# Keys turned in blocks by VectorE and brought to their tokens by GpSimd's transfers, held until the matrix to be inverted has been loaded

## The chip, the cores and the metric

The kernel runs on one core of one Trainium2 chip. A core has five engines that run their own instruction streams in order: TensorE (PE, matmuls, with its weight loads on PEld), VectorE (DVE), ScalarE (ACT), GpSimd (POOL) and SyncE (SP), besides the DMA engines that carry transfers between memories. The metric is the device time of one execution in microseconds (us); a run's verdict is taken from the medians of several executions. The time before is a median of 2228.72 us over 3 runs (2228.09 to 2231.8).

## The reference, cut to what matters

One step of a hybrid backbone: an RMS norm, one wide input projection, a bidirectional RWKV-7 time mixing over 32 heads of size 64 with 128 context and 256 latent tokens, beside it a gated short convolution, then the output projections. The part that the change touches is the time mixing. Per head and direction a 64x64 state S runs over the tokens:

```python
def step(S, inp):
    r_t, w_t, k_t, v_t, a_t, b_t = inp
    sa = jnp.einsum('dbhij,dbhj->dbhi', S, a_t)
    S = S * w_t[..., None, :] + sa[..., :, None] * b_t[..., None, :] + v_t[..., :, None] * k_t[..., None, :]
    y = jnp.einsum('dbhij,dbhj->dbhi', S, r_t)
    return S, y
...
S_fin, ys = _wkv_bidir(S0, _heads(r2), _heads(decay), _heads(k_dir), _heads(v2),
                       _heads(-kk2), _heads(kk2 * a))
```

The kernel doesn't step through single tokens. It cuts the 384 tokens of a direction into chunks of 64, computes within a chunk with matrices of 64x64 (one of them has to be inverted), and carries the state from chunk to chunk.

## The kernel before, in words

Everything large is a dense matmul with the weights read from HBM: 1 MB arrives as a tile `raw` (line 101 on), ACT casts it to a rounded high part `whi` (L88), DVE subtracts to get the low part `wlo` (L89), and each product is three matmuls (L81, L82, L83). The class `Stream` hands these dense steps out one at a time (`ds_.go(n)`, n steps of 3 matmuls).

Between the dense steps stand 16 blocks b, of two heads (128 columns) each. A block runs through `prep_a` (projections of decay and rates), `prep_k` (keys, logarithms of decay, exponentials), `prep_b`, `prep_c`, `scan`, `norm` and `finish`. Each function is a generator, and what it yields is the number of dense steps that PE does at that place (the function `drive`). So PE's order is written out by hand (`tc.manual_schedule` for PE alone). The order of the other engines is chosen by a scheduler when the program is built, from priorities (the scan has 300 more) and its own estimate of when an operand is there. On the chip each engine runs its list in that fixed order.

One block, with its lines:

- `prep_b` multiplies the keys and bonus keys with decays, `bk0`/`bk1` (two DVE products per direction, the lines under L679) and `pr0`/`pr1`. PE makes the chunk matrices `pA` (L708), DVE masks them into `A` (L714). Four corners go out through DRAM (`ui`, L719), come back with one matrix per partition as `un` (L732) and `ux` (L734). The loop at L737 to L742 inverts them on DVE in 30 steps of two instructions each. The inverse goes out (`uo`, L746), into `A` (L752), and is turned to `x11` (L755).
- Meanwhile POOL multiplies `bk` with the end decay (L722), DVE turns the values in 32x32 blocks (`vt`, L727), and `prep_c` brings these blocks with 8 POOL transfers to their tokens, the lower half of `sav` (L777). PE turns the keys with 10 transposes through PSUM (`pb`, L784) and ACT copies them into `bt` (L785, four copies).
- `scan` does `pav`, `pH`, `pX` (L862, L854), which complete the inverse, and then runs two chains over the chunks. One step of a chain is: PE `pq` (L833), ACT copies it into `sav` (L835), PE `pu` with `bt` and `sav` (L840), DVE puts it into the state `st` (L843 for a chain's first step from zero, L845 otherwise), PE `po` from `st` (L816), DVE adds it into `sav` (L817). The chains alternate with 2 or 4 dense steps between.
- Inside the scan, after the copies of `pX` into `A` (L890), the function `keys` calls `prep_k` of the next block: reciprocals (L651), `kn` (L652), two running sums `L_0`, `L_1` (L659), exponentials on ACT (L661, L662), `kd` (L664, L665) and `sig` (L666).

Of the kernel before, what the change touches and what calls it, by code (L numbers as in the profile page):

```python
# [9 lines left out]
F32 = mybir.dt.float32  # L10
F32R = mybir.dt.float32r
AF = mybir.ActivationFunctionType
ALU = mybir.AluOpType
AX = mybir.AxisListType

P = 128
# [5 lines left out]
C = 64  # L22
NCH = 6
# [33 lines left out]
def hybrid_step(ctx, tc, cst, x_prompt, x_sample, state_f, state_b, c, c_ctx, ada_w, ada_b, norm_g,  # L57
# [3 lines left out]
    V, S, G, TE = nc.vector, nc.scalar, nc.gpsimd, nc.tensor  # L61
# [14 lines left out]
    ident = cs[:, C_ID:C_ID + P]  # L76
# [150 lines left out]
    for i in range(3):  # L227
        pr = pp.tile([P, P], F32, tag=f"prow{i}", name=f"prow{i}")
# [24 lines left out]
    def pcol(i, n=1):  # L253
        return par[:, i:i + n]
# [154 lines left out]
    def tmp(nm):  # L409
        return box["sp"].tile([P, T], F32, tag="t", name=nm, bufs=8)  # L410
# [134 lines left out]
    sp = ctx_sc.enter_context(tc.tile_pool(name="sp", bufs=1))  # L545
# [6 lines left out]
    for i in range(3):  # L552
        t = tmp(f"lst_{i}")
# [4 lines left out]
    for m in range(4):  # L558
# [6 lines left out]
        t = tmp(f"lin_{m}")  # L565
# [16 lines left out]
    for i in range(4):  # L582
        ep = sp.tile([P, NCH, C + 1], F32, tag=f"ep{i}", name=f"ep{i}")
# [6 lines left out]
    def bank(nm):  # L590
        return ps1.tile([P, 4, P], F32, tag="A", name=nm, bufs=5)

    def c3(a):
        return a.rearrange("p (n t) -> p n t", t=C)

    def flat(a):
        return a.rearrange("p n t -> p (n t)")
# [11 lines left out]
    ux = sp.tile([112, 16, 32], F32, tag="ux", name="ux")  # L609
# [62 lines left out]
    def prep_b(b, o):  # L672

        r, kk = r_[b], o["kk"]
        o["pr"], o["bk"] = [], []
        for d in range(2):
            ep, em, kd, bn = o["ep"][d], o["em"][d], o["kd"][d], o["bn"][d]
            pr = sp.tile([P, NCH, P], F32, tag=f"pr{d}", name=f"pr_{b}_{d}")
            bk = sp.tile([P, NCH, P], F32, tag=f"bk{d}", name=f"bk_{b}_{d}")  # L679
            V.tensor_tensor(bk[:, :, 0:C], c3(bn[:]), c3(em[:]), ALU.mult)  # L680
            V.tensor_tensor(bk[:, :, C:P], c3(kd[:]), c3(em[:]), ALU.mult)
            V.tensor_tensor(pr[:, :, 0:C], c3(kk[:, ::-1] if d else kk[:]), ep[:, :, 0:C], ALU.mult)
            r3 = c3(r[:])
            if d == 0:
                V.tensor_tensor(pr[:, :, C:P], r3, ep[:, :, 1:C + 1], ALU.mult)
            else:
                V.tensor_tensor(pr[:, :, C:P], r3[:, ::-1, :], ep[:, :, C:0:-1], ALU.mult)
            o["pr"].append(pr)
            o["bk"].append(bk)
        yield PB0  # L690

        def blocks(A, d, e):

            es = slice(32 * e, 32 * e + 32)
            return A[es, 0, NCH * d:NCH * d + NCH, :].rearrange("s n (h t) -> s (n h) t", h=2)[:, :, es]

        ui = dp.tile([2, 2, 12, 32, 32], F32, tag="ui", name=f"ui_{b}", bufs=2)
        uo = dp.tile([2, 2, 12, 32, 32], F32, tag="uo", name=f"uo_{b}", bufs=2)

        A = sp.tile([P, 2, 2 * NCH, P], F32, tag="A", name=f"A_{b}")  # L700
        o["A"] = A
        for d in range(2):
            pr, bk = o["pr"][d], o["bk"][d]
            m0 = C_MB if d else C_MF
            pas = {(h, n0): bank(f"pA_{b}_{d}_{h}_{n0}") for n0 in (0, 4) for h in range(2)}
            for n in range(NCH):
                for h in range(2):
                    TE.matmul(pas[h, n // 4 * 4][:, n % 4, :], bk[hss[h], n, :], pr[hss[h], n, :],  # L708
                              start=True, stop=True)
            for n0, w in ((0, 4), (4, 2)):  # L710
                mk = cs[:, m0:m0 + P].rearrange("p (w t) -> p w t", t=C).unsqueeze(1).broadcast_to([P, w, 2, C])
                for h in range(2):
                    f0 = NCH * d + n0
                    last = V.tensor_tensor(A[:, :, f0:f0 + w, hss[h]].rearrange("p w n t -> p n w t"),  # L714
                                           pas[h, n0][:, 0:w, :].rearrange("p n (w t) -> p n w t", t=C), mk,
                                           ALU.mult).ins
            yield PB1
            for e in range(2):
                nc.sync.dma_start(ui[d, e].rearrange("i s t -> s i t"), blocks(A, d, e))  # L719

        for d in range(2):
            G.tensor_tensor(o["bk"][d][:], o["bk"][d][:], o["ep"][d][:, :, C:C + 1].broadcast_to([P, NCH, P]), ALU.mult)  # L722

        vt = sp.tile([P, 2, T], F32, tag="vt", name=f"vt_{b}")
        with tc.issue_after(last):
            for d in range(2):
                V.transpose(vt[:, d], v_[b][:, ::-1] if d else v_[b][:])  # L727
        o["vt"] = vt


        for g in range(2):
            nc.sync.dma_start(un[64 * g:64 * g + 48], ui[:].rearrange("d e i s t -> (d e i) s t"))  # L732
        for g in range(2):
            nc.sync.dma_start(ux[64 * g:64 * g + 48],  # L734
                              ui[:].rearrange("d e i (m g) t -> (d e i) m g t", g=2)[:, :, g, :])
        ut = sp.tile([112, 128], F32, tag="ut", name=f"ut_{b}")
        for s in range(1, 31):  # L737
            w, m = 31 - s, (s + 1) // 2
            tv = ut[:, 0:m * w].rearrange("p (a b) -> p a b", b=w)
            V.tensor_tensor(tv, ux[:, 0:m, s:s + 1].broadcast_to([112, m, w]),  # L740
                            un[:, s:s + 1, s + 1:].broadcast_to([112, m, w]), ALU.mult)
            V.tensor_tensor(ux[:, 0:m, s + 1:], ux[:, 0:m, s + 1:], tv, ALU.add)  # L742
        for g in range(2):
            dg = ux[64 * g:64 * g + 48].rearrange("p a b -> p (a b)")[:, g:512:34]
            V.tensor_scalar(dg, dg, 1.0, None, ALU.add)
            nc.sync.dma_start(uo[:].rearrange("d e i (m g) t -> (d e i) m g t", g=2)[:, :, g, :],  # L746
                              ux[64 * g:64 * g + 48])
        x11 = un[0:64, 0:24, :]
        o["x11"] = x11
        for e in range(2):  # L750
            for d in range(2):
                nc.sync.dma_start(blocks(A, d, e), uo[d, e].rearrange("i s t -> s i t"))  # L752

        for d in range(2):
            box["turned"] = V.transpose(x11[0:32, 12 * d:12 * d + 12, :], blocks(A, d, 0)).ins  # L755

    def prep_c(b, o):

        r = r_[b]

        s_in = sp.tile([P, 2, C], F32, tag="s_in", name=f"s_in_{b}")
        for d in range(2):
            for h in range(2):
                for jb in range(2):
                    p0 = C * h + 32 * jb
                    nc.sync.dma_start(s_in[p0:p0 + 32, d, :].rearrange("i (b j) -> i b j", j=32),
                                      ctx_st[d][0, 0, 2 * b + h].rearrange("(b i) j -> i b j", i=32)
                                      [:, :, 32 * jb:32 * jb + 32])

        sav = sp.tile([P, 2 * NCH, P], F32, tag="sav", name=f"sav_{b}")  # L770
        bt = sp.tile([P, 2 * NCH, P], F32, tag="bt", name=f"bt_{b}")
        o["sav"], o["bkt"] = sav, bt

        x = o["vt"][:].rearrange("p d (n e t) -> p (d n) e t", e=2, t=32)
        for e in range(2):
            for q in range(4):
                G.dma_start(sav[C + 32 * e:C + 32 * e + 32, :, 32 * q:32 * q + 32], x[32 * q:32 * q + 32, :, e, :])  # L777
        yield 2
        for d in range(2):

            for n0, n1 in (((0, 4), (4, 5)), ((0, 3), (4, 6)))[d]:
                pb = bank(f"pb_{b}_{d}_{n0}")
                for n in range(n0, n1):
                    TE.transpose(pb[:, n - n0, :], o["bk"][d][:, n, :], ident)  # L784
                S.copy(bt[:, NCH * d + n0:NCH * d + n1, :], pb[:, 0:n1 - n0, :])  # L785
                yield 1
        ks = o["kd"]
        V.tensor_tensor(ks[0][:], ks[0][:], ks[1][:, ::-1], ALU.add)
        V.scalar_tensor_tensor(ks[0][:], ks[0][:], pcol(RK + b), r[:], ALU.mult, ALU.mult)
        o["bsum"] = hl_parts(ks[0], sp.tile([P, T], F32R, tag="t", name=f"bsh_{b}", bufs=8), f"bs_{b}")  # L790
        yield 1
        for h in range(2):
            for d in range(2):
                V.transpose(st[1][hss[h], d, hss[h]], s_in[hss[h], d, :])
# [178 lines left out]
    for b in range(NB):  # L973
# [10 lines left out]
        n = drive(prep_c(b, cur))  # L984
# [140 lines left out]
    for half in range(2):  # L1125
# [8 lines left out]
        for s in range(3):  # L1134
# [10 lines left out]
            if half == 1:  # L1145
                f = rsf[:, s, :]
# [37 lines left out]
```

## Time and profile before

| what | value |
|---|---|
| median of 3 runs | 2228.72 us |
| the profiled execution's own time | 2230.84 us |
| its span in the trace | 2229.1 us |
| DVE busy | 1501.9 us (67%) |
| ACT busy | 978.4 us (44%) |
| POOL busy | 200.9 us (9%) |
| start of block 3, of block 4 | 520.83, 625.14 us |

The span is what the trace covers; the execution's own time has another 1.7 us around it. The blocks start at 185.36 us (block 0) and 1773.00 us (block 15), and those from 2 to 14 are 103.7 to 105.5 us apart. Groups of instructions are read as: line, engine, operation, output from input, count, busy time in us, mean ns of one, and idle time of the engine just before them with what ended it.

### The profile page before, as it was taken

How to read it: one execution, taken by the hardware profiler on the slowest of the kernel's cores; microseconds unless marked ns; L12 is line 12 of the kernel's file. 1: busy time of each engine (PE TensorE's matmuls, PEld its weight loads, DVE VectorE, ACT ScalarE, POOL GpSimd, SP SyncE). 2: the span in 40 equal slices, each digit the busy share in tenths (PEclk: the TensorE clock that was granted, in tenths of full speed). 3: DMA queues.
4: the chain of work that ended last, by engine and by line, in shares of the span. 5: the costliest groups of instructions: out<-in, count | busy, mean ns of one | idle time of the engine just before them, and what ended most of it. 6: DMA issues, size and time to landing. Idle time of an engine off the chain costs nothing.

```text
span 2229.1 us, 40796 instructions
## 1 busy us (share of the span) xinstructions
PE 2168.6 (97%) x15924; PEld 2056.5 (92%) x15924; DVE 1501.9 (67%) x3288; ACT 978.4 (44%) x1704; POOL 200.9 (9%) x243
## 2 busy tenths in 40 slices
PE   6999999999999999999999999999999999999998
PEld 3588999999999999999999999999999999898988
DVE  3248567786877777868768786877777775444354
ACT  4245435453535454444436353536353634333333
POOL 2001010101010101111010101010101010000000
PEclk9999999999999999999999999999999999999999
DMA  9975464546464536364554546364546474887633
GB/s 337 346 213 131 142 144 128 126 108 146 107 147 107 133 108 143 112 144 105 138 115 128 126 108 146 108 145 124 138 121 153 147 206 146 292 273 234 219 132 114
DMA packets 480850, 347.88 MB, mean 156 GB/s; under 512 B 134720, under 2 KB 460944, under 8 KB 479760
## 3 DMA queue, kind: packets, MB, share of 16 engines
q1 hardware_dynamic: 475072, 337.20, 54.2%
q0 software_dynamic: 5152, 6.49, 2.0%
q8 instruction: 126, 2.06, 0.4%
q10 hardware_dynamic: 432, 1.57, 0.2%
q14 instruction: 68, 0.56, 0.1%
HBM read 312.09 MB, written 26.21 MB: 152 GB/s over the span
## 4 chain that ended last, share of the span: by engine, by line
PE 72%; DVE 13%; DMA 7%; ACT 3%; issue 2%; SPq 1%; POOL 0%; ACTq 0%; POOLq 0%; DVEq 0%
DMA raw_adah<-in_ada_w_dram 4%; PE d_rk L81 3%; PE d_rk L83 3%; PE d_rk L82 3%; PE d_gv L81 3%; PE d_gv L82 3%; PE d_gv L83 3%; PE pA L708 2%; PE d_oa L81 2%; PE d_oa L83 2%; PE d_oa L82 2%; PE d_bc L81 2%; PE d_mb L81 2%; PE d_gb L81 2%; PE d_mb L82 2%
## 5 line engine op out<-in xcount | busy, mean ns | idle before, releaser
L81 PE MATMUL d_rk<-h_hi,whi_rk 128*128 128x384 f32 x480 | 161.5, 337 | 0.6 <-ACT lst L554 0.6
L81 PE MATMUL d_gv<-h_hi,whi_gv 128*128 128x384 f32 x480 | 161.1, 336 | 0.0
L82 PE MATMUL d_gv<-h_lo,whi_gv 128*128 128x384 f32 x480 | 160.8, 335 | 0.0
L83 PE MATMUL d_gv<-h_hi,wlo_gv 128*128 128x384 f32 x480 | 160.7, 335 | 0.0
L83 PE MATMUL d_rk<-h_hi,wlo_rk 128*128 128x384 f32 x480 | 160.4, 334 | 0.0
L82 PE MATMUL d_rk<-h_lo,whi_rk 128*128 128x384 f32 x480 | 160.4, 334 | 0.0
L740 DVE TENSOR_TENSOR ut<-ux,un 112x30 f32<-112x30 f32 (+7 forms) x480 | 119.3, 248 | 16.6 <-DMA ux<-ui 4.2
L742 DVE TENSOR_TENSOR ux<-ux,ut 112x30 f32<-112x30 f32 (+7 forms) x480 | 119.3, 249 | 13.6
L88 ACT CAST whi_gv<-raw_gv 128x1024 fp32r<-128x1024 f32 (+1 forms) x64 | 64.0, 999 | 139.5 <-PE d_gv L82 34.0
L88 ACT CAST whi_rk<-raw_rk 128x1024 fp32r<-128x1024 f32 x60 | 62.9, 1052 | 119.1 <-PE d_rk L82 37.9
L89 DVE TENSOR_TENSOR wlo_rk<-raw_rk,whi_rk 128x1024 fp32r<-128x1024 f32 x60 | 73.1, 1221 | 50.0 <-ACT whi_rk L88 50.0
L81 PE MATMUL d_ob<-ybh,whi_ob 128*128 128x384 f32 x256 | 88.8, 347 | 3.8 <-ACT whi_ob L88 3.1
L81 PE MATMUL d_bg<-h_hi,whi_bg 128*128 128x384 f32 x256 | 91.8, 359 | 0.0
L81 PE MATMUL d_bc<-h_hi,whi_bc 128*128 128x384 f32 x256 | 91.7, 358 | 0.0
L81 PE MATMUL d_gb<-h_hi,whi_gb 128*128 128x384 f32 x256 | 91.7, 358 | 0.0
L81 PE MATMUL d_bx<-h_hi,whi_bx 128*128 128x384 f32 x256 | 91.5, 358 | 0.0
L81 PE MATMUL d_ma<-h_hi,whi_ma 128*128 128x384 f32 x256 | 91.0, 356 | 0.0
L81 PEld LDWEIGHTS d_rk<-h_hi,whi_rk 128*128 128x128 f32 x480 | 90.1, 188 | 0.9 <-ACT lst L554 0.9
L81 PEld LDWEIGHTS d_gv<-h_hi,whi_gv 128*128 128x128 f32 x480 | 90.4, 188 | 0.2
L82 PEld LDWEIGHTS d_gv<-h_lo,whi_gv 128*128 128x128 f32 x480 | 90.6, 189 | 0.0
L83 PEld LDWEIGHTS d_gv<-h_hi,wlo_gv 128*128 128x128 f32 x480 | 90.5, 188 | 0.0
L81 PE MATMUL d_mb<-h_hi,whi_mb 128*128 128x384 f32 x256 | 90.2, 352 | 0.0
(313 smaller groups left out, 6595.4 us busy)
## 6 DMA issues: line engine op xcount, KB each, us to landing
raw_adah<-in_ada_w_dram SPq DMA_DIRECT2D x64, 512.0 KB, 8.7
raw_rk<-in_w_in_dram SPq DMA_DIRECT2D x60, 512.0 KB, 5.3
raw_gv<-in_w_in_dram SPq DMA_DIRECT2D x60, 512.0 KB, 5.6
raw_ma<-in_w_in_dram SPq DMA_DIRECT2D x16, 1024.0 KB, 5.5
raw_mb<-in_w_in_dram SPq DMA_DIRECT2D x16, 1024.0 KB, 5.5
raw_bc<-in_w_in_dram SPq DMA_DIRECT2D x16, 1024.0 KB, 5.4
raw_bx<-in_w_in_dram SPq DMA_DIRECT2D x16, 1024.0 KB, 5.4
raw_bg<-in_w_in_dram SPq DMA_DIRECT2D x16, 1024.0 KB, 5.5
```

The lines of the kernel that those rows point to most:

```text
L81: TE.matmul(out, wh, xh, start=start, stop=False)
L82: TE.matmul(out, wh, xl, start=False, stop=False)
L83: TE.matmul(out, wl, xh, start=False, stop=stop)
L88: S.copy(hi[0:rows], src)
L89: V.tensor_tensor(lo[0:rows], src, hi[0:rows].bitcast(F32), ALU.subtract)
L708: TE.matmul(pas[h, n // 4 * 4][:, n % 4, :], bk[hss[h], n, :], pr[hss[h], n, :], start=True, stop=True)
L740: V.tensor_tensor(tv, ux[:, 0:m, s:s + 1].broadcast_to([112, m, w]), un[:, s:s + 1, s + 1:].broadcast_to([112, m, w]), ALU.mult)
L742: V.tensor_tensor(ux[:, 0:m, s + 1:], ux[:, 0:m, s + 1:], tv, ALU.add)
```

## The change

`bk0` and `bk1` become one tile `bks` with both directions. DVE turns it in place in 32x32 blocks, two instructions of 128x768 behind those for `vt`. PE's transposes `pb` and ACT's copies into `bt` are gone; in their place POOL issues 16 transfers per block, one for each 32x32 block position, from `bks` into `bt`. A one-element POOL copy `mark` reads `ux`, so it waits for that load; the 8 transfers into `sav` and the 16 into `bt` are issued after it. The dense steps that PE does there are 6 in both (2 and four times 1 before).

```diff
--- before.py
+++ after.py
@@ -672,11 +672,13 @@
     def prep_b(b, o):
 
         r, kk = r_[b], o["kk"]
-        o["pr"], o["bk"] = [], []
+        o["pr"] = []
+        bks = sp.tile([P, 2, NCH, P], F32, tag="bk", name=f"bk_{b}")
+        o["bk"] = [bks[:, d] for d in range(2)]
         for d in range(2):
             ep, em, kd, bn = o["ep"][d], o["em"][d], o["kd"][d], o["bn"][d]
             pr = sp.tile([P, NCH, P], F32, tag=f"pr{d}", name=f"pr_{b}_{d}")
-            bk = sp.tile([P, NCH, P], F32, tag=f"bk{d}", name=f"bk_{b}_{d}")
+            bk = o["bk"][d]
             V.tensor_tensor(bk[:, :, 0:C], c3(bn[:]), c3(em[:]), ALU.mult)
             V.tensor_tensor(bk[:, :, C:P], c3(kd[:]), c3(em[:]), ALU.mult)
             V.tensor_tensor(pr[:, :, 0:C], c3(kk[:, ::-1] if d else kk[:]), ep[:, :, 0:C], ALU.mult)
@@ -686,7 +688,6 @@
             else:
                 V.tensor_tensor(pr[:, :, C:P], r3[:, ::-1, :], ep[:, :, C:0:-1], ALU.mult)
             o["pr"].append(pr)
-            o["bk"].append(bk)
         yield PB0
 
         def blocks(A, d, e):
@@ -719,13 +720,15 @@
                 nc.sync.dma_start(ui[d, e].rearrange("i s t -> s i t"), blocks(A, d, e))
 
         for d in range(2):
-            G.tensor_tensor(o["bk"][d][:], o["bk"][d][:], o["ep"][d][:, :, C:C + 1].broadcast_to([P, NCH, P]), ALU.mult)
+            G.tensor_tensor(bks[:, d], bks[:, d], o["ep"][d][:, :, C:C + 1].broadcast_to([P, NCH, P]), ALU.mult)
 
         vt = sp.tile([P, 2, T], F32, tag="vt", name=f"vt_{b}")
         with tc.issue_after(last):
             for d in range(2):
                 V.transpose(vt[:, d], v_[b][:, ::-1] if d else v_[b][:])
-        o["vt"] = vt
+            for d in range(2):
+                V.transpose(flat(bks[:, d]), flat(bks[:, d]))
+        o["bks"], o["vt"] = bks, vt
 
 
         for g in range(2):
@@ -771,19 +774,21 @@
         bt = sp.tile([P, 2 * NCH, P], F32, tag="bt", name=f"bt_{b}")
         o["sav"], o["bkt"] = sav, bt
 
+        mark = sp.tile([1, 1], F32, tag="mark", name=f"mark_{b}")
+        mark = G.tensor_copy(mark[:], ux[64:65, 0, 1:2]).ins
         x = o["vt"][:].rearrange("p d (n e t) -> p (d n) e t", e=2, t=32)
         for e in range(2):
             for q in range(4):
-                G.dma_start(sav[C + 32 * e:C + 32 * e + 32, :, 32 * q:32 * q + 32], x[32 * q:32 * q + 32, :, e, :])
-        yield 2
-        for d in range(2):
-
-            for n0, n1 in (((0, 4), (4, 5)), ((0, 3), (4, 6)))[d]:
-                pb = bank(f"pb_{b}_{d}_{n0}")
-                for n in range(n0, n1):
-                    TE.transpose(pb[:, n - n0, :], o["bk"][d][:, n, :], ident)
-                S.copy(bt[:, NCH * d + n0:NCH * d + n1, :], pb[:, 0:n1 - n0, :])
-                yield 1
+                with tc.issue_after(mark):
+                    G.dma_start(sav[C + 32 * e:C + 32 * e + 32, :, 32 * q:32 * q + 32],
+                                x[32 * q:32 * q + 32, :, e, :])
+        x = o["bks"][:].rearrange("p d n t -> p (d n) t")
+        for p in range(4):
+            for q in range(4):
+                with tc.issue_after(mark):
+                    G.dma_start(bt[32 * p:32 * p + 32, :, 32 * q:32 * q + 32],
+                                x[32 * q:32 * q + 32, :, 32 * p:32 * p + 32])
+        yield 6
         ks = o["kd"]
         V.tensor_tensor(ks[0][:], ks[0][:], ks[1][:, ::-1], ALU.add)
         V.scalar_tensor_tensor(ks[0][:], ks[0][:], pcol(RK + b), r[:], ALU.mult, ALU.mult)
```

The lines below `prep_b` move by 1 to 5 in the changed file (L843 becomes L848, L845 L850, L835 L840, L890 L895).

In the rows below a name with `_b` numbers is a tile (its last number only tells one use from another), and `x2` counts equal instructions in a row. First, the list of DVE before, in the scan of block 3, from the copies into `A` to the first states; `st_1144` is the state of one chain and `st_1146` that of the other:

```order
L890 COPY A_5058<-pX_5762 32x6x32 x2
L651 RECIPROCAL kn_5657<-kn_5657 128x128 x3
L659 SCALAR_TENSOR_TENSOR L_0_5807<-cs,sig_0_5598 128x384
L89 TENSOR_TENSOR wlo_bg_0_1_5748<-raw_bg_0_5741,whi_bg_0_1_5747 128x1024
L843 COPY st_1144<-pu_0_0_5845 64x2x64 x2
L652 SCALAR_TENSOR_TENSOR kn_5657<-kk_5562,kn_5657 128x384
L664 TENSOR_SCALAR kd_0_5811<-sig_2_5634,par,omka 128x384
L845 TENSOR_TENSOR st_1146<-pu_1_0_5863,ls_1_0_5733 64x2x64 x2
```

Here the state copies come as the fifth row, and most of the next block's keys behind them. The same place of DVE in the changed kernel, from the row behind the reciprocals on:

```order
L659 SCALAR_TENSOR_TENSOR L_0_5811<-cs,sig_0_5602 128x384
L652 SCALAR_TENSOR_TENSOR kn_5661<-kk_5566,kn_5661 128x384
L664 TENSOR_SCALAR kd_0_5815<-sig_2_5638,par,omka 128x384
L659 SCALAR_TENSOR_TENSOR L_1_5819<-cs,sig_1_5614 128x384
L665 TENSOR_TENSOR kd_0_5815<-k_5428,kd_0_5815 128x384
L666 TENSOR_TENSOR sig_2_5638<-kn_5661,sig_2_5638 128x384
L664 TENSOR_SCALAR kd_1_5823<-sig_3_5650,par,omka 128x384
L665 TENSOR_TENSOR kd_1_5823<-k_5428,kd_1_5823 128x384
L666 TENSOR_TENSOR sig_3_5650<-kn_5661,sig_3_5650 128x384
L682 TENSOR_TENSOR bk_6145<-sig_2_5638,sig_0_5602 128x6x64
L683 TENSOR_TENSOR bk_6145<-kd_0_5815,sig_0_5602 128x6x64
```

and directly behind these rows, still DVE in the changed kernel:

```order
L682 TENSOR_TENSOR bk_6145<-sig_3_5650,sig_1_5614 128x6x64
L683 TENSOR_TENSOR bk_6145<-kd_1_5823,sig_1_5614 128x6x64
L793 TENSOR_TENSOR kd_0_5815<-kd_0_5815,kd_1_5823 128x384
L794 SCALAR_TENSOR_TENSOR kd_0_5815<-kd_0_5815,par,r_5408 128x384
L89 TENSOR_TENSOR wlo_bg_0_1_5752<-raw_bg_0_5745,whi_bg_0_1_5751 128x1024
L848 COPY st_1144<-pu_0_0_5849 64x2x64 x2
```

All of the next block's `prep_k`, the four products `bk` of its `prep_b` and the two of its `prep_c` (L793, L794) now stand ahead of the state copies. It is the same in blocks 2 to 14. In block 1 `prep_k` stands ahead, but not the products; in block 0 the order is as before, and block 15 has no next block.

On ACT, at the same place of the changed kernel, from the copies into `A` on:

```order
L895 COPY A_5060<-pX_5766 32x6x32 x2
L661 ACT_TABLE_LOAD
L661 ACTIVATE ep_1148<-L_0_5811 128x6x64
L662 ACTIVATE sig_0_5602<-L_0_5811 128x384
L661 ACTIVATE ep_1150<-L_1_5819 128x6x64
L662 ACTIVATE sig_1_5614<-L_1_5819 128x384
L840 COPY sav_5243<-pq_0_0_5827 64x2x64 x2
```

The four exponentials of the next block now stand ahead of the copies of the first `pq`; before, those copies stood ahead of all of them.

On POOL, in the changed kernel, the list of one block:

```order
L723 TENSOR_TENSOR bk_1423<-bk_1423,ep_1148 128x768
L723 TENSOR_TENSOR bk_1423<-bk_1423,ep_1150 128x768
L778 COPY mark_1677<-ux 1x1
L783 DMA sav_1675<-vt_1586 32x12x32 x8
L789 DMA bt_1676<-bk_1423 32x12x32 x16
L880 MEMSET A_1493 64x1536
```

The copy `mark` is new, the 8 transfers into `sav` stand behind it now, and the 16 into `bt` are new.

## The prediction

> **What bounds the kernel now.** The first view is the page's list of busy times, and its forty slices.
>
> ```profile
> PE 2168.6 (97%) x15924; PEld 2056.5 (92%) x15924; DVE 1501.9 (67%) x3288; ACT 978.4 (44%) x1704; POOL 200.9 (9%) x243
> ...
> PE   6999999999999999999999999999999999999998
> ...
> PEclk9999999999999999999999999999999999999999
> ```
>
> PE is busy in nine tenths or more of nearly every slice, at a full granted clock. So PE's list of work is the time: an instruction taken from PE is a gain, a microsecond for which PE stands is a loss, and the work of DVE, ACT, POOL and the DMA counts only where PE comes to wait for it. Since PE's list is fixed, I look in the waits for how near that is.
>
> ```profile
> PE po L816 <- DVE st L845: 7.8, 9, 1.6
> PE pu L840 <- ACT sav L835: 1.5, 6, 0.3
> ```
>
> The columns are us in total, times, and the longest. PE waits only 9 times for a state and 6 times for the copies of `pq`, in 16 blocks. But the places are tight, so I read the timeline of PE at the first states of block 3.
>
> ```profile
> 588.36 0.61 PE L840 MATMUL pu<-sav,bt 128*128 128x128 f32 x4
> ...
> 591.34 0.61 PE L816 MATMUL po<-st,pr 128*128 128x128 f32 x4
> ```
>
> Columns: start, us, instruction. From the first `pu` to the first `po` there are 2.98 us, filled with dense steps. In this time DVE has to make the state.
>
> **Removed from PE: the transposes.** The group of the ten transposes per block, and PE's timeline where four of them stand between dense matmuls:
>
> ```profile
> L784 PE MATMUL pb<-cs,bk 128*128 128x128 f32 x160 | 28.0, 273 | 0.9 <-DVE A L714 0.8
> ```
>
> ```profile
> 195.26 0.33 PE L81 MATMUL d_ma<-h_hi,whi_ma 128*128 128x384 f32 x1
> ...
> 197.17 0.34 PE L83 MATMUL d_ma<-h_hi,wlo_ma 128*128 128x384 f32 x1
> 197.34 0.60 PE L784 MATMUL pb<-cs,bk 128*128 128x128 f32 x4
> 197.70 0.42 PE L81 MATMUL d_ma<-h_hi,whi_ma 128*128 128x384 f32 x1
> 197.96 0.34 PE L82 MATMUL d_ma<-h_lo,whi_ma 128*128 128x384 f32 x1
> ```
>
> Durations overlap, since matmuls are pipelined, so I count starts. Eleven dense steps lie from 195.26 to 197.17: 0.174 us each. From 197.17 to 197.96 there are two dense steps and four transposes: 0.79 - 0.35 = 0.44 us, 0.11 per transpose. 160 x 0.11 = **17.6 us** less PE work. This lies on the path, since PE is the path. The dense steps stay six, so nothing is put in its place.
>
> **Removed from ACT**: 64 copies into `bt`. ACT has time there and PE reads `bt` only in the scan's `pu`. Nothing.
>
> **Moved on DVE: the next block's keys stand ahead of the states.** This is the largest term, and it isn't in the diff: only the order of instructions shows it. The timeline of DVE from 585.33 us on (block 3, before) has a start for each of these instructions:
>
> ```profile
> 585.33 2.55 DVE L651 RECIPROCAL kn<-kn 128x128 f32<-128x128 f32 x3
> 587.82 0.88 DVE L659 TENSOR_TENSOR_SCAN L<-cs,sig 128x384 f32<-128x384 f32 x1
> 588.63 1.19 DVE L89 TENSOR_TENSOR wlo_bg<-raw_bg,whi_bg 128x1024 fp32r<-128x1024 f32 x1
> 589.84 0.59 DVE L843 COPY st<-pu 64x128 f32<-64x128 f32 x2
> 590.47 0.56 DVE L652 SCALAR_TENSOR_TENSOR kn<-kk,kn 128x384 f32<-128x384 f32 x1
> 590.94 0.47 DVE L664 TENSOR_SCALAR kd<-sig,par,omka 128x384 f32<-128x384 f32 x1
> 591.45 0.59 DVE L845 TENSOR_TENSOR st<-pu,ls 64x128 f32<-64x128 f32 x2
> 592.07 0.56 DVE L665 TENSOR_TENSOR kd<-k,kd 128x384 f32<-128x384 f32 x1
> 592.55 0.55 DVE L666 TENSOR_TENSOR sig<-kn,sig 128x384 f32<-128x384 f32 x1
> 593.13 0.42 DVE L817 TENSOR_TENSOR sav<-po,sav 64x256 f32<-64x256 f32 x1
> 593.47 0.94 DVE L659 TENSOR_TENSOR_SCAN L<-cs,sig 128x384 f32<-128x384 f32 x1
> 594.33 0.45 DVE L664 TENSOR_SCALAR kd<-sig,par,omka 128x384 f32<-128x384 f32 x1
> 594.71 0.54 DVE L467 TENSOR_TENSOR bc<-bc,d_bx 128x384 f32<-128x384 f32 x1
> ...
> 595.50 0.54 DVE L665 TENSOR_TENSOR kd<-k,kd 128x384 f32<-128x384 f32 x1
> 595.97 0.55 DVE L666 TENSOR_TENSOR sig<-kn,sig 128x384 f32<-128x384 f32 x1
> ```
>
> Before, the state copy starts 4.51 us after the reciprocals do (585.33 to 589.84) and is done at 590.43, 0.91 us ahead of `po` at 591.34. DVE runs without a pause there, so an instruction that comes in ahead pushes the state back by its distance from start to start. In the new order, from 585.33 on: reciprocals 2.49, `L_0` 0.81, `kn` 0.47, `kd` 0.51, `L_1` 0.86, `kd` 0.48, `sig` 0.47, `kd` 0.38, `kd` 0.47, `sig` 0.47; sum 7.41 (`sig` from start to start as the `kd` ahead of it, 595.50 to 595.97). Then the products of `prep_b` and `prep_c`:
>
> ```profile
> L680 DVE TENSOR_TENSOR bk<-sig,sig 128x384 f32<-128x384 f32 x32 | 17.6, 549 | 0.0
> ...
> L789 DVE SCALAR_TENSOR_TENSOR kd<-kd,par,r 128x384 f32<-128x384 f32 x16 | 9.8, 615 | 0.4
> ```
>
> An instruction of 0.55 us on 384 elements takes 0.47 from start to start in the rows above. Four `bk` and the sum of `kd` are 5 x 0.47 = 2.35, the last `kd` 0.615 - 0.08 = 0.54; then `wlo_bg` with 1.21. Together 7.41 + 2.35 + 0.54 + 1.21 = **11.5 us** against 4.51. So the states start at 596.84 and are done at 597.43. Where PE waited for a state, it started about 0.13 us behind its end: in block 3 later, the state's pair is done at 602.14 and `po` starts at 602.29.
>
> ```profile
> 601.55 0.59 DVE L845 TENSOR_TENSOR st<-pu,ls 64x128 f32<-64x128 f32 x2
> ```
>
> ```profile
> 602.29 0.68 PE L816 MATMUL po<-st,pr 128*128 128x128 f32 x4 [0.78 <-DVE st L845]
> ```
>
> `po` would start at 597.56 instead of 591.34: PE stands for **6.2 us**. Queued behind these rows on DVE are only this chain's states and sums; the only one that waits for them is PE, which has no other work in its list.
>
> **Moved on ACT: the exponentials stand ahead of the copies of `pq`.**
>
> ```profile
> 586.07 0.55 ACT L835 COPY sav<-pq 64x128 f32<-64x128 f32 x2 [1.05 <-PE pq L833]
> ...
> 588.51 1.28 ACT L661 ACT_TABLE_LOAD   x1
> 589.80 0.53 ACT L661 ACTIVATE ep<-L 128x384 f32<-128x384 f32 x1
> ```
>
> The table load needs no operand. `L_0` ends at 588.7 and `L_1` at about 590.5 in the new order; two exponentials of 0.53 behind `L_1` give 591.5, and the copy of `pq` is done at 592.1 instead of 586.6. So `pu` comes at about 592.2 instead of 588.36, a stall of 3.8 us. It lies within the 6.2: `po` comes 2.98 us of filling behind `pu`, at 595.2, and the state's copy is later still. It isn't counted twice. The exponentials of the first direction are done long before DVE needs them for `bk` at 592.7. If DVE did not have the longer list, ACT alone would cost 3.8 us per block.
>
> **How often.** Blocks 2 to 14 have this order: 13 x 6.2 = 80.6 us. Block 1 has `prep_k` and `wlo` ahead, without the products: 7.41 + 1.21 = 8.62 against 4.51, less the slack of 0.91 (and the 0.13): 3.3 us. Blocks 0 and 15 nothing. Sum **83.9 us**. What comes back: later in the scan DVE has less to do, so the nine waits for states, 7.8 us, mostly go; I take 5 of them.
>
> **Added: DVE's turns.** The two turns of `vt` are the nearest rows, with the wait behind which they stand:
>
> ```profile
> 528.78 1.03 DVE L727 STREAM_TRANSPOSE vt<-v 128x384 f32<-128x384 f32 x2
> 530.10 1.23 DVE L89 TENSOR_TENSOR wlo_rk<-raw_rk,whi_rk 128x1024 fp32r<-128x1024 f32 x1 [0.29 <-ACT whi_rk L88]
> ...
> 541.55 0.18 DVE L745 TENSOR_SCALAR ux<-ux 48x16 f32<-48x16 f32 x1 [5.22 <-DMA ux<-ui]
> ```
>
> 768 elements are twice 384: 1.03 us each, 2.1 us per block. DVE's last idle stretch before `ux` has come (541.55) is 5.22 us, which covers them. Nothing; without that cover 2.1 us per block on the inverse.
>
> **Added and moved: POOL's copy and 24 transfers.**
>
> ```profile
> L777 POOL DMA_DIRECT2D sav<-vt x128 | 79.2, 626 | 32.1 <-ACT whi_rk L88 16.7 <-DVE lo_bs L605 8.2 <-DVE vt L727 4.3
> ...
> sav<-vt POOLq DMA_DIRECT2D x128, 48.0 KB, 6.5
> ```
>
> An issue takes 0.62 us, so 24 take 14.9; landing is 6.5 later in the median. From 541.5 that is 563; `pu` reads `bt` at 588.36. 25 us of slack: nothing. Queued behind on POOL is only the memset of `A` that stands behind `pH`. The bounds: by the transfer's share (2.0% of the 16 engines for 128 of them, 0.34 us each) 24 fill 8 us of all engines, ahead of `uo`, which leaves after the loop. If one ran into the return of the inverse, a wait of 0 to 2 us per block; and without the 8 `sav` transfers beside them `un` and `ux` come earlier. Since PE reaches `pH` 1.1 us earlier, the inverse must come as much earlier or PE waits; I bound this with 0 to 1.1 us per block, 0 to 17 in all, and take 0, since `ux` now travels alone.
>
> [...] The inverse's loop would stand beside the 24 issues all the time. [...]
>
> **The sum.** 2230.84 (profiled) - 17.6 + 83.9 - 5 = 2292. The profiled run is 2.1 us above the median of the runs, 2228.72, so I say **2290** on that basis.
>
> **Rivals.**
>
> 1. *The gain comes through*: the moved keys cost PE nothing, because the list ahead of the states is short enough or its operands early enough. The point: the list would have to be at most 4.51 + 0.91 + 1.35 = 6.8 us long instead of 11.5 to end even (1.35 is 17.6 over 13 blocks). Against: DVE's rows there run back to back, none waits. Time: 2228.7 - 17.6 - 0 to 5, about 2209. Chance 0.10.
> 2. *Half of it*: instructions of 384 elements run faster in their new places, or PE's filling moves, so that the stall is about 2 us. 26 + 1 - 18 - 5, within a few us of before. Chance 0.05.
> 3. *POOL's issues stretch beside DVE*, as they stand beside the loop. From (588.36 - 541.5 - 6.5) / 24 = 1.7 us per issue on, `bt` is late and PE waits: at 2 us 7.5 us per block more, 2290 + 120. Against: 694 ns was the longest of 128. Chance 0.03.
> 4. *The inverse is late* through the new transfers, on top of the forecast: up to 17 us, 2307. Chance 0.12, within the range.
>
> **How the numbers follow.** Forecast (with rival 4 within) 0.82, of which the price per block of the stall is from 4.8 (if instructions overlap better) to 7.5 us (if the exponentials come late for `bk`): 2270 to 2307, and with rival 4 to 2315. To keep no more than 2 in 10 outside I set 2255 to 2316. About 0.2% (4.5 us) can be told from no change: slower 0.84, same 0.04, faster 0.12.
>
> **What will show it.** In the trace of after: `po` (now L821) waiting for `st` (L848), about 6 us in each of blocks 2 to 14, 3 in block 1, and none in 0 and 15; `pu` waiting for the copies of `pq` as part of it; blocks 5 us longer; no rows of `pb`; issues of 0.62 us with `bt` landed before 565 in block 3. I am wrong if PE shows none of these waits, or if PE waits for `bt` or for `x11`.

## The result, and the profile after

The changed kernel takes 2345.89 us (median of 4 runs, 2343.97 to 2347.02), the one before, beside it, 2230.22 us. The ratio is 1.0518, 95% interval 1.05 to 1.0537: 5.2% slower. The forecast was 2290 us; the direction is right, the loss is nearly twice as large as forecast, and the time lies outside the range. Mean periods of blocks 2 to 14 (from the starts of `pA`, `pH` and the first `pu` in PE's timeline) say where it is:

| stretch of a block, mean of blocks 2 to 14, us | before | after |
|---|---|---|
| first `pA` to first `pH` | 57.11 | 58.19 |
| first `pH` to first `pu` | 10.45 | 16.17 |
| first `pu` to the end | 36.81 | 38.46 |
| block | 104.38 | 112.82 |

13 x 8.44 = 110 us of the 116.1 us by which the span grew (2229.1 to 2345.2); block 1 has another 4.9.

The page of the changed kernel, busy times:

```profile
span 2345.2 us, 40719 instructions
...
PE 2207.9 (94%) x15764; PEld 2093.6 (89%) x15764; DVE 1531.2 (65%) x3320; ACT 939.7 (40%) x1628; POOL 359.8 (15%) x515
```

PE has 160 instructions less and is busy for 39 us more than before (2168.6). And it stands more: its waits after (us in total, times, longest),

```profile
PE pu L845 <- ACT sav L840: 36.0, 13, 3.2
...
PE po L821 <- DVE st L848: 13.9, 12, 2.4
PE pav L867 <- DMA sav<-vt: 10.2, 10, 3.2
PE pav L867 <- DMA bt<-bk: 7.1, 6, 2.3
PE pH L859 <- issue: 6.5, 6, 1.7
...
PE pq L838 <- POOL A L880: 4.5, 2, 2.8
```

The first two were forecast, though not with these sizes: PE waits at `pu` in blocks 1 to 3 and 5 to 14, at `po` in blocks 1 to 6 and 8 to 13. The waits at `pav`, `pH` and `pq` were not. (`pav` reads `sav` and `A`, not `bt`. The issues into `sav` and `bt` use the same eight semaphores in turn, so the view can put the name of the one for the other; in blocks 2 to 11, where `pav` waits, its last wait ends about 0.25 us after the last of the 8 transfers into `sav` has landed.) They lead to POOL. Its timeline in block 3 of the changed kernel, which starts at 533.22 us:

```profile
576.68 0.17 POOL L778 COPY mark<-ux 1x1 f32<-1x1 f32 x1 [35.33 <-DVE ux L748]
577.19 4.95 POOL L783 DMA_DIRECT2D sav<-vt  x8 [0.34 <-issue]
582.13 0.61 POOL L789 DMA_DIRECT2D bt<-bk  x1
583.71 1.23 POOL L789 DMA_DIRECT2D bt<-bk  x2 [0.96 <-DMA sav<-vt]
...
596.69 1.83 POOL L789 DMA_DIRECT2D bt<-bk  x3 [0.69 <-DMA bt<-bk]
```

and VectorE's timeline there:

```profile
576.38 0.18 DVE L748 TENSOR_SCALAR ux<-ux 48x16 f32<-48x16 f32 x1
```

The mark comes 43.5 us after the block's start, not at about 20. Its releaser isn't the load of `ux`, but VectorE's last addition to the diagonal of `ux` (L748), just before the loop's end. The code explains it: the mark copies `ux[64:65, 0, 1:2]` (one element of partition 64), and for the second group (partitions from 64) the diagonal begins at element 1. So the mark reads the one element of that row that the inversion writes at its end, and the wait is that of a reader for the last writer.

### The profile page after: what moved, and what is told of

It reads as the page before. It is cut to its first block, busy times and chain, and to the rows that moved or that the text cites. A ratio compares the mean times of both kernels' runs of the same rounds, so it can differ in the third digit from the quotient of the medians.

```text
span 2345.2 us, 40719 instructions
## 1 busy us (share of the span) xinstructions
PE 2207.9 (94%) x15764; PEld 2093.6 (89%) x15764; DVE 1531.2 (65%) x3320; ACT 939.7 (40%) x1628; POOL 359.8 (15%) x515
## 4 chain that ended last, share of the span: by engine, by line
PE 66%; DVE 15%; DMA 11%; issue 3%; ACT 2%; SPq 1%; POOL 1%; DVEq 0%; POOLq 0%; ACTq 0%
DMA raw_adah<-in_ada_w_dram 3%; PE d_rk L81 3%; PE d_rk L82 3%; PE d_rk L83 3%; PE pA L709 2%; PE d_oa L81 2%; DMA uo<-ux 2%; PE d_oa L83 2%; PE d_oa L82 2%; DVE ux L745 2%; DVE ut L743 2%; PE d_gv L81 2%; PE d_gv L82 2%; PE d_gv L83 2%; PE po L821 2%
## 5 line engine op out<-in xcount | busy, mean ns | idle before, releaser
L789 POOL DMA_DIRECT2D bt<-bk x256 | 156.4, 616 | 95.2 <-DMA bt<-bk 47.1
L946 POOL TENSOR_TENSOR rs<-var,nhalf 128x6 f32<-128x6 f32 x16 | 21.6, 1352 | 674.6 <-DVE var L944 674.6
L845 PE MATMUL pu<-sav,bt 128*128 128x128 f32 x320 | 56.9, 306 | 36.0 <-ACT sav L840 36.0
```

The lines of the kernel that those rows point to most:

```text
L789: G.dma_start(bt[32 * p:32 * p + 32, :, 32 * q:32 * q + 32], x[32 * q:32 * q + 32, :, 32 * p:32 * p + 32])
L845: TE.matmul(pu[:, d, :], bt[:, f, :], sav[:, f, :], start=True, stop=True)
L946: G.tensor_tensor(rs[:], var[:], nhalf[:], ALU.pow)
```

## Experiments

Unless it says otherwise, each is the changed kernel with the edit shown. "Early" means that the mark waits for the load, "late" for the end of the loop; "keys first" and "states first" are the two orders on VectorE in the scan.

### e1: the mark reads element 0

```diff
-        mark = G.tensor_copy(mark[:], ux[64:65, 0, 1:2]).ins
+        mark = G.tensor_copy(mark[:], ux[64:65, 0, 0:1]).ins
```

> The mark copies element 0 of that row of ux instead of element 1. Only the load of ux writes element 0; element 1 lies on the diagonal and is written once more by VectorE at the end of the inversion's loop. Theory A (the whole loss of 116 us hangs on the late mark: the transfers leave 23 us too late, and the scheduler, which sees that, puts the next block's keys ahead of the states): mark at about 19 to 21 us of a block instead of 44, keys again behind the first states, no waits of PE for sav at pav or for the copies of pq, and 17.6 us less than before: 2205 to 2216 us. Theory B (transfers beside the loop cost more than they save): issues of over 1.7 us, or the loop ending over 1 us later than 45.5 us: 2240 us or more. Theory C (the keys' order is the loss, whenever the transfers leave): about 2290.

2208.03 us, ratio to before 0.9907 (0.9892 to 0.9922): 138 us less than the changed kernel, by one index. With this index the scheduler put the states first again by itself. POOL's timeline in block 3 (start 513.83):

```profile
532.52 0.26 POOL L778 COPY mark<-ux 1x1 f32<-1x1 f32 x1 [10.55 <-DMA ux<-ui]
533.38 4.95 POOL L783 DMA_DIRECT2D sav<-vt  x8 [0.61 <-DVE ut L743]
540.33 5.47 POOL L789 DMA_DIRECT2D bt<-bk  x9 [2.00 <-DMA sav<-vt]
548.78 4.26 POOL L789 DMA_DIRECT2D bt<-bk  x7 [2.97 <-DMA bt<-bk]
```

The mark's releaser is now the load, 18.7 us after the block's start. All 24 issues stand beside VectorE's loop, and the loop still ends at 44.4 us of a block in the mean. A block takes 103.05 us, 1.33 less than before. Theory A holds, B and C fall.

### e2, e3, e8: the two effects apart

e2 keeps the late mark and puts the next block's keys, but for the reciprocals and the first sum, behind the first states and the first copies of `pq` (the 7 calls `keys` later in the scan, when these exist):

```diff
+        hold = ExitStack()
+        for x in first:
+            hold.enter_context(tc.issue_after(x))
         V.scalar_tensor_tensor(kn[:], kk[:], -1.0, kn[:], ALU.mult, ALU.mult)
...
+        hold.close()
...
-                prep_k(b + 1, nxt)
+                prep_k(b + 1, nxt, cur["first"])
...
-        drive(scan(b, cur), 300, 3 if b < NB - 1 else None, keys)
+        drive(scan(b, cur), 300, 7 if b < NB - 1 else None, keys)
```

> The mark stays as in the changed kernel (late), but the next block's keys behind the reciprocals and the first sum stand behind the first states again. Theory A (two costs beside each other: 6 us per block from the keys' order, the rest from late transfers): 2346 - 13 x 6.0 - 3 = about 2265, at most 2285 if pu then waits for bt itself; PE still waits at pav for sav and at pH. Theory B (the order is nearly all): 2211 to 2225. Theory C (the late transfers are nearly all, since pu would wait for bt at the same place): 2320 to 2346.

2275.4 us (1.0206, 1.0187 to 1.0224), between the two numbers of theory A. e8 is its control, the same forced order with e1's mark:

> Control for e2: the same forced order of keys behind the first states, but with the early mark. If forcing the order costs nothing by itself: as e1, 2203 to 2213, and all of e2's 67 us are due to the late transfers. If it costs: above 2215, and e2 counts for less.

2203.47 us (0.9894, 0.9879 to 0.9909). The order costs nothing by itself; it even gains 5 us on e1, since PE's waits of `po` for states fall from 7.5 to 2.8 us. So the late transfers alone cost 2275.4 - 2203.5 = 72 us. About half of it is standing. In e2 PE waits 18.6 us in all at `pav` and 9.7 at `pH`, and a third place comes in:

```profile
PE pq L845 <- POOL A L891: 6.1, 5, 2.1
```

This is the memset of `A` that stands behind the 16 issues in POOL's list and goes late with them. The rest is in PE itself: it is busy for 2179.4 us in e2 and 2146.3 in e8, 33 us more for the same 15764 instructions (see e9 to e11).

e3 has e1's early mark and forces the keys first:

```diff
-                            V.tensor_copy(st[ch][hs, :, hs], pu[hs, 0:2, hs])
+                        with tc.issue_after(o["keys_next"]) if i == 0 and "keys_next" in o else ExitStack():
+                            ...
...
                 prep_k(b + 1, nxt)
+                if b > 1:
+                    keys_bk(b + 1, nxt)
+                    cur["keys_next"], cur["exp_next"] = nxt["kdone"], nxt["exp"]
```

(`keys_bk` holds the four products `bk` and the two of `kd`; the first copies of `pq` are put behind `exp_next` in the same way.)

> Early mark as in e1, but the keys, the products bk and kd of the next block and the exponentials are forced ahead of the first states and of the first copies of pq, in blocks 2 to 14, as they stand in the changed kernel. This is the world that the prediction took for granted. Theory A: e1 + 13 x 6.2 = about 2290, PE standing some 6 us per block between pq and the first po. Rival: PE's clock falls after each stand and its dense work gets longer: 2300 to 2320.

2290.75 us (1.0279, 1.0261 to 1.0296). It is the world of the prediction, and almost exactly its time. A block takes 109.07 us, 6.02 more than in e1; 6.2 was forecast. The waits of PE in e3:

```profile
PE pu L854 <- ACT sav L849: 60.0, 14, 4.6
```

The stand shows at `pu`, behind the exponentials on ScalarE, and not at `po`, where the sum had put it. PE's timeline of block 3:

```profile
595.97 1.22 PE L854 MATMUL pu<-sav,bt 128*128 128x128 f32 x4 [4.61 <-ACT sav L849]
598.91 0.85 PE L854 MATMUL pu<-sav,bt 128*128 128x128 f32 x4
600.88 0.68 PE L829 MATMUL po<-st,pr 128*128 128x128 f32 x4
```

From `pu` to `po` there are 4.91 us instead of 2.98, because PE's filling runs slower after the stand: its dense steps take 0.32 us from start to start between the two rows of `pu` (597.31 to 598.59), and 0.17 to 0.18 before the stand and from 599.78 on. In blocks 2 and 3 `po` starts 0.15 us behind the end of the state's copies, so there the state still ends the stretch, as in the sum. In blocks 4 to 14 it doesn't: the state is done 0.4 to 1.15 us before PE comes to `po`. Block 14, VectorE and PE:

```profile
1799.55 0.61 DVE L858 COPY st<-pu 64x128 f32<-64x128 f32 x2
```

```profile
1801.29 0.61 PE L829 MATMUL po<-st,pr 128*128 128x128 f32 x4
```

There the wait for ScalarE and the slower filling set the time, and VectorE's list, which is nearly as long, stands hidden beside them. So what the rival said of the clock is in the trace, though not its time: PE is busy for 2176.1 us in e3 against 2143.8 in e1, with the same 15764 instructions, and the mean granted clock is 0.978 against 0.997. e3 forces VectorE's and ScalarE's order together; no run prices one of them alone.

The four cells, in us:

| | states first | keys first |
|---|---|---|
| early mark | 2208 (e1), 2203 (e8) | 2291 (e3) |
| late mark | 2275 (e2) | 2346 (the change) |

With the early mark the keys' order costs 83 us; the late mark costs 72 with the states first. Together they cost 138 to 142, some 15 us less than their sum.

### e5, e6: which of the late transfers

e5 lets the 8 transfers into `sav` go early and holds the 16 into `bt` late, e6 the other way; both with e2's order.

```diff
+        early = G.tensor_copy(early[:], ux[64:65, 0, 0:1]).ins
...
-                with tc.issue_after(mark):
+                with tc.issue_after(early):
                     G.dma_start(sav[...
+        late = G.tensor_copy(late[:], ux[64:65, 0, 1:2]).ins
...
-                with tc.issue_after(mark):
+                with tc.issue_after(late):
                     G.dma_start(bt[...
```

> Splits the 67 us between e1 and e2 (late transfers, states first): the 8 transfers into sav leave early, after the load, only the 16 into bt wait for the loop's end. No wait of PE at pav for sav. If the collision of the transfers with the way of the inverse (uo, then A) is the cost, 16 of 24 transfers keep most of it: x11 at 57 to 59 us of a block, PE waiting at pH, 2240 to 2265. If the late sav is the cost: 2208 to 2220.

> The other part: the 16 transfers into bt leave after the load, the 8 into sav wait for the loop's end (44 us of a block) and land at about 55, where PE's pav stands at 54.4. If late sav is the cost: PE waits 1 to 3 us per block at pav, 2230 to 2255. If the collision with 16 transfers is the cost: at most 2225.

e5: 2281.83 us (1.0245, 1.023 to 1.0261), more than expected, and even more than e2 with all 24 late. e6: 2255.83 us (1.0119, 1.0102 to 1.0136), just above the range for a late `sav`. Against e8, whose lists of VectorE and ScalarE are the same, that is 78 and 52 us: each part alone does most of the harm of both, so they don't add. The waits of PE in e5, and then in e6:

```profile
PE pH L873 <- issue: 49.9, 14, 6.1
```

```profile
PE pav L881 <- DMA sav<-vt: 17.6, 14, 3.5
PE pav L881 <- issue: 8.6, 6, 2.1
```

In e5 the transfers into `bt` fall right on the way of the inverse: `x11` is turned at 59.9 us of a block in the mean, against 54.5 in e8, where `pav` and `pH` stand at 54.4 and 56.0. The row of `pH` names no releaser, but the timelines of VectorE and PE do (block 3; `x11` is a part of the tile `un`, the first of its two turns takes half of the row's time):

```profile
584.29 1.03 DVE L765 STREAM_TRANSPOSE un<-A 32x384 f32<-32x384 f32 x2 [8.21 <-DMA A<-uo]
```

```profile
584.96 0.96 PE L873 MATMUL pH<-un,A 32*32 32x32 f32 x48 [5.97 <-issue]
```

The turn waits for the returned inverse, and `pH` starts 0.10 us behind the first turn's end in each of blocks 2 to 14. In e6 `pav` waits for the lower half of `sav`, which it reads; but `x11` is late there too (58.4 us), so the 8 transfers slow the inverse as well. In e2 `x11` comes at 58.5, earlier than in e5. That the 8 into `sav`, which go first, hold the 16 back and soften the collision would fit this, but no run shows it. The median times from issue to landing, before, then after, then e1:

```profile
uo<-ux SPq DMA_DIRECT2D x32, 96.0 KB, 2.9
A<-uo SPq DMA_DIRECT2D x64, 48.0 KB, 4.7
```

```profile
uo<-ux SPq DMA_DIRECT2D x32, 96.0 KB, 5.4
A<-uo SPq DMA_DIRECT2D x64, 48.0 KB, 6.2
```

```profile
uo<-ux SPq DMA_DIRECT2D x32, 96.0 KB, 3.7
A<-uo SPq DMA_DIRECT2D x64, 48.0 KB, 3.3
```

The way of the inverse takes 11.6 us after and 7.0 in e1 (sums of the two medians); the slack of `x11` before `pH` is 1.5 us in the mean of e1's blocks 2 to 14.

### e4, e7: what the hold is worth

e4 has no mark: all 24 are issued as soon as their blocks are turned. e7 is e1 with the hold only on the 16 into `bt`.

```diff
-        mark = sp.tile([1, 1], F32, tag="mark", name=f"mark_{b}")
-        mark = G.tensor_copy(mark[:], ux[64:65, 0, 1:2]).ins
...
-                with tc.issue_after(mark):
-                    G.dma_start(sav[...
+                G.dma_start(sav[...
```

> No mark: the 8 and 16 transfers are issued as soon as the values and keys are turned, so beside the loads of un and ux. Theory A (the hold is worth something): ux lands 1 to 3 us later than before, x11 comes too late for pH (its slack before was 0.2 to 2.1 us, less the 1.1 us by which PE is earlier), PE waits 1 to 3 us per block: 2225 to 2250. Rival (the transfers don't disturb the loads): as e1, 2205 to 2216.

> As e1, but the 8 transfers into sav are issued without the hold, as before the change. e4 lost 42 us against e1 with all 24 beside the loads of un and ux. If the 8 do their share of it (a third): 2215 to 2228, ux landing 1 to 2 us later than in e1. If only the 16 into bt do harm, or the slack at pH of 1.9 us covers it: 2206 to 2211.

e4: 2250.56 us (1.0102, 1.0087 to 1.0117), at the upper end of theory A; e7: 2213.09 us (0.9938, 0.9923 to 0.9953), between its two ranges. So the hold until the load is worth 42 us, and for the 8 into `sav` alone 5. The loss in e4 isn't only the later `ux` (8.3 us to landing against 5.6 in e1). The wait that grew most is ScalarE's in e4:

```profile
ACT whi_gv L88 <- DMA raw_gv<-in_w_in_dram: 147.8, 22, 10.1
```

The weights that are queued at that time land after 10.2 us instead of 5.3; their cast is late, and VectorE, which has the low part of these weights in the middle of the loop's list, stands for it: the loop takes 27.8 us instead of 25.7 (means of blocks 2 to 14). PE itself waits 15.0 us in e4 for VectorE's `ga` (L440) and 7.6 for its `lwl`; in e1 it is 0 and 1.7.

### e9, e10, e11: standing and PE's clock

In the changed kernel PE's busy time grew though its work shrank. Windows of 4 us in its block 3 (length; busy time and count of PE, PEld, DVE, ACT and POOL; PEclk, the clock granted to PE as a share of the full one; DMA share; GB/s):

```profile
586.00:590.00 4.00, 2.58 (x32) 2.18 (x32) 0.33 (x1) 0.58 (x1) 3.01 (x5) 1.00 1.34 156
590.00:594.00 4.00, 4.00 (x86) 3.82 (x83) 2.29 (x5) 1.00 (x3) 2.50 (x5) 0.50 1.14 267
594.00:598.00 4.00, 4.00 (x19) 4.00 (x18) 0.42 (x1) 2.40 (x5) 1.93 (x4) 0.64 0.99 138
```

After the wait at `pav` (1.16 us in this block) the granted clock is 0.50 in one window and 0.64 in the mean of the next. e9 and e10 fill the stand of e5 with work whose result is not used:

```diff
+        if 1 < b < NB - 1:
+            fill = bank(f"fill_{b}")
+            for _ in range(24):
+                TE.matmul(flat(fill[:, 0:3, :]), bones_r[:], o["bsum"][0][:], start=True, stop=True)
```

> e5 with 24 useless matmuls (128x384, 4.2 us at full clock, their result is never read) in each of blocks 2 to 14, where PE stands for the late inverse, between pav and pH. If standing also costs the clock that PE has afterwards: the stretch from pH to the first pu falls from 12.0 to 13.3 us to about 10.5, and the time falls, although PE has 13 x 4.2 = 54 us more work: 2255 to 2274. If the stands alone cost, nothing is won, and blocks whose stand was shorter than 4.2 us get longer: 2282 to 2296.

2309.27 us (1.0372, 1.0355 to 1.039), above both ranges. It decides nothing: the scheduler had moved ScalarE's cast of `lraw`, which waits for a transfer, ahead of the copies of `pH`, and PE then stood at `pX` and `pq`. e10 and e11 put that cast behind these copies and have the same order on ScalarE and VectorE; e11 has no filling.

```diff
-                with tc.issue_after(box["kn"]) if m == 0 and "kn" in box else ExitStack():
+                with tc.issue_after(box["kn"]) if m == 0 and "kn" in box else ExitStack(), \
+                        tc.issue_after(box["xs"]) if m == 0 and "xs" in box else ExitStack():
```

> e9's answer was spoilt by an order: in 8 of its blocks ScalarE's cast of lraw, which waited for a transfer, had come ahead of the copies of pH. Here that cast is put behind them in all blocks, with the same 24 useless matmuls. Against e11, which is the same without them: if standing costs PE's clock afterwards, the dense steps behind pH run at 0.17 us from start to start instead of 0.32, a gain of 1 to 1.5 us in each block whose stand is over 4.2 us, less 2 to 3 us in each block with a stand of 1 to 2 us: 5 to 10 us below e11 in all. If the clock costs nothing that isn't hidden: 0 to 15 us above e11.

> Control for e10: e5 with ScalarE's cast of lraw behind the copies of pH in all blocks, no useless matmuls. As e5, 2270 to 2285.

e10: 2274.33 us (1.021, 1.0195 to 1.0225); e11: 2279.51 us (1.0229, 1.0212 to 1.0246). With 13 x 4.2 = 54 us more matmuls e10 is 5 us below e11 by the medians, as expected. The four times of each don't overlap (2273.1 to 2277.3 against 2278.1 to 2283.2), but the intervals of the two ratios do, so the total is a hint, and the timelines carry the point. PE behind the stand in block 3, e11:

```profile
586.26 0.96 PE L874 MATMUL pH<-un,A 32*32 32x32 f32 x48 [4.63 <-issue]
587.15 0.69 PE L81 MATMUL d_bx<-h_hi,whi_bx 128*128 128x384 f32 x1
587.64 0.52 PE L82 MATMUL d_bx<-h_lo,whi_bx 128*128 128x384 f32 x1
587.96 0.52 PE L83 MATMUL d_bx<-h_hi,wlo_bx 128*128 128x384 f32 x1
```

and e10:

```profile
586.09 0.80 PE L874 MATMUL pH<-un,A 32*32 32x32 f32 x48 [0.72 <-issue]
586.82 0.44 PE L81 MATMUL d_bx<-h_hi,whi_bx 128*128 128x384 f32 x1
587.10 0.34 PE L82 MATMUL d_bx<-h_lo,whi_bx 128*128 128x384 f32 x1
587.27 0.34 PE L83 MATMUL d_bx<-h_hi,wlo_bx 128*128 128x384 f32 x1
```

0.32 us from start to start against 0.17; the stretch from `pH` to the first `pu` is 12.42 us in this block of e11 and 10.58 in e10 (10.45 in the mean before the change). In e11 the granted clock falls to 0.50 in each of blocks 2 to 14, in e10 in none of them; its mean over the profiled execution is 0.977 in e11 and 0.994 in e10. In these two runs the lower clock goes with the stand, and work without use takes it away.

## Why the prediction was right in part and wrong in size

- **Removed from PE**: 17.6 us forecast; e1 is 2228.85 - 2208.03 = 20.8 us faster than the runs before beside it. The stretch from `pA` to `pH`, where the transposes stood, is 55.96 us in e1 instead of 57.11: 1.15 per block against 1.10 forecast. Right; the other 2 us are not traced to a cause.
- **The keys ahead of the states**: right in place and in the length of VectorE's list. From the start of the reciprocals to the end of the state's copies the changed kernel takes 12.2 us in blocks 2 to 14 and 9.2 in block 1 (forecast: 11.5 + 0.59 = 12.1, and 8.62 + 0.59 = 9.2), and `po` starts 0.14 to 0.19 us behind that (forecast 0.13). What it costs, 6.2 us per block and 2290 in all, is close to what e3 measures with the early mark: 6.0 and 2290.75. That the keys' order costs this is shown by e3, which differs from e1 by the order alone. But the price is right partly by luck. In e3 PE stands 4.6 us at `pu` for ScalarE (3.8 forecast, and taken as hidden), and then its slower filling, which the sum doesn't have, ends the stretch in 11 of 13 blocks instead of the state. And e3 leaves out block 1, for which the total holds 3.3 us.
- **The step that failed** is the one on POOL's copy and transfers: "From 541.5 that is 563; `pu` reads `bt` at 588.36. 25 us of slack: nothing." It let the mark go when `ux` had been loaded. The mark reads an element that the loop's last instruction on the diagonal writes, and goes 23 us later. With that the transfers meet the return of the inverse, `sav` misses `pav`, and the memset behind them misses `pq`: 55 us more than e3 in the changed kernel, 72 us by itself (e2 against e8). PE never comes to wait for `bt` at `pu`, the one place that this step weighed: in block 3 the last of `bt` lands at 67.4 us of the block, and `pu` starts at 74.4.
- The bound for a wait at the inverse, 0 to 17 us in all, was kept for transfers that had the loop's time to themselves; rival 4 was so the right mechanism at the wrong price. That the change might not do what its name says was not among the rivals. It should have been: the order of the keys was itself a sign. e1 shows that the late mark made the scheduler move them; that it did so because it expected `bt`, which `pu` reads, to be late is the likely way, and not shown. The prediction took the moved order without asking what made it move.
- **POOL's issues beside DVE** (rival 3): not seen. In e1 all of them stand beside the loop, and the list of one line's instructions says

```profile
L789 POOL DMA_DIRECT2D bt<-bk x256: 615/615/624, 209.9 to 1802.0; - x128
```

ns, smallest, median and largest; the rival needed 1700 or more.
- **The turns on VectorE** cost nothing in e1, whose loop ends earlier than before (44.4 against 45.9 us of a block): as forecast.
- That stands are followed by a slower PE was not in the sum. For the same 15764 instructions PE is busy for 2143.8 us in e1, 2176.1 in e3 and 2207.9 in the changed kernel. In e3 most of this lies in time that PE would have stood for the state anyway; behind `pH` it lengthens the way to `pu` (12.42 against 10.58 us in e11 and e10).

## What to carry to other kernels

An instruction that only marks a moment waits for the last writer of what it reads (in block 3 the mark went at 43.5 us, behind VectorE, with element 1, and at 18.7, behind the load, with element 0): choose an element that no later step writes, and look at what the marker waits for in the built program. When a scheduler has reordered something that a change didn't mention, first find which operand it takes to be late; the cause may be there, and cost more than the reordering. Transfers that are moved out of one load's way must be placed against the next transfer on the path too: here the way of the inverse took 11.6 us beside the late ones and 7.0 in e1.

## What the runs showed of the hardware

Behind a stand of 4.63 us PE's dense steps took 0.32 us from start to start instead of 0.17, until the clock rose again 4.5 us after the stand's end (e11, block 3, granted clock 0.50 from 583.95 to 590.78 us). With matmuls of no use in the stand the granted clock was 1.00 all the time from 578.91 to 602.91 us (e10, block 3). In the traces of before and of the changed kernel the stretches at 0.50 are 3.41, 6.83 or 10.24 us long, but for the one at the end of each trace. A stand as long as that in e11 was not needed for it: in block 3 of the changed kernel the clock fell at 590.03, and in the 3.41 us before that PE was busy for 1.99.

The 24 issues of POOL don't run through in 14.9 us: in e1's rows above they stop twice for earlier transfers (2.00 and 2.97 us), and take 19.7 us from the first to the last. That is the program's doing and not the chip's: in the trace each issue from the ninth on waits for the semaphore of the one eight issues ahead (in block 3 of the changed kernel that is so for all 16 into `bt`).
